# All low halves of expert and u-table pages, and the index one-hot products, on VectorE

## The chip, the cores and the metric

The program runs on one core of a Trainium2 chip. The metric is the device time of one execution in microseconds (us), from the first to the last instruction; less is better. The engines are named as in the profile: PE is TensorE's matmuls and PEld its weight loads, DVE is VectorE, ACT is ScalarE, POOL is GpSimd, SP is SyncE, which issues most DMAs.

## The reference

Two layers on 512 tokens of 1024 features, in float32 (cut to what the change touches):

```python
# layer 1, second half: mixture of 32 experts, 4 for each token
def expert_block(args):
    xe, e = args
    gu = xe @ w_gate_up[e] + b_gate_up[e]
    g = jnp.minimum(gu[:, :D_FF], SWIGLU_LIMIT)
    u = jnp.clip(gu[:, D_FF:], -SWIGLU_LIMIT, SWIGLU_LIMIT)
    act = (u + 1.0) * (g * jax.nn.sigmoid(SWIGLU_ALPHA * g))
    return act @ w_down[e] + b_down[e]
...
# layer 2, second half: 8 heads, 16 of 128 * 128 small experts for each head of a token
cand_i = (i_top[..., 0, :, None] * PEER_KEYS + i_top[..., 1, None, :]).reshape(bsz, seq, PEER_HEADS, PEER_TOPK * PEER_TOPK)
best_s, pos = lax.top_k(cand_s, PEER_TOPK)
expert_idx = jnp.take_along_axis(cand_i, pos, axis=-1)
gates = jax.nn.softmax(best_s, axis=-1)
...
u_sel = u_tab[i_blk]
act = jax.nn.gelu(jnp.einsum('td,thkd->thk', h_blk, u_sel).astype(jnp.float32))
w = (g_blk * act).astype(h.dtype)
return jnp.einsum('thk,thkd->td', w, v_tab[i_blk])
```

Before and after these stand attention layers and a state-space branch, which the change doesn't touch.

## The kernel before

All weights come as pages of 128 x 1024 float32 (512 KB). A product of two float32 matrices is made of three matmuls on halves that the matrix engine takes exactly: `WStream` (L196) loads a page `wr` by a DMA on SP, ACT writes its high half `wh` (`split1`, L217), and another engine writes the low half, `wl = wr - wh` (`low`, L232). The stream's argument `eng` says which engine that is for page number i; None is VectorE. `mm3` (L167) multiplies high by high, high by low and low by high. `get` (L265) hands out the next pair, loads ahead and splits ahead, so that for each page used one later page is split.

**Expert stage** (`phase2`, L1375). 32 places of the stream follow each other, 24 pages to a place (16 of gate and up, 8 of down): 768 pages in order of use (`expert_stream`, L1349). Loops run over the place `e`, over three parts of 8 pages and over the page; a table `sched` puts the other work (gathering an expert's rows, transposing them, the activation `swiglu`, the output `y`) after given pages. `gu` and `dn` are the products' PSUM tiles. The low half of every sixth page goes to GpSimd (L1372). GpSimd also issues the gather of the rows (`xg`, L1244) and the scatter of the results (`ybuf`, L1317).

**U-table stage** (first part of `phase4`, L2213). For three of four blocks of tokens (384 tokens) every small expert's product is made: 128 pages of the u table, 24 matmuls each (`uchunk`, L2297; PSUM tile `ft`, then a gelu on ACT into `us`, which is stored). Between them stand 16 pages of the queries, the choice of the best pairs (`select`, L2320), and `gates` (L2387): from the chosen indices `rt` it builds one-hot matrices `oa` and `oB` on DVE (and one part of `oB` on ACT) whose product `G` spreads the gates over the table; a step of it is 4 tokens, and there are 96. In `select` the position of each best pair is turned into a one-hot tensor `oh`, multiplied with the candidates' indices `ci` (128 x 800), and summed into `ex`. For the last block of tokens the rows are gathered instead (`gathered`, L2445, tiles `ug`, sums in `x`), by indirect DMAs on GpSimd.

The order of these lanes is set by `race` (L99): a `Clock` (L33) adds up estimated costs of what has been emitted for each engine, and the lane that comes due first emits its next step. `Clock.either` (L42) picks VectorE or GpSimd by that estimate and a bias (`VB`, `VB2` = 4.0, 1.0 us against VectorE, L1018); it chose the engine for the low halves of u pages (L2238) and for the product of `oh` and `ci` (L2352). As soon as `race` is over, the last 11 u pages are emitted, then the v-table stage (`vphase`, L2504), in which GpSimd multiplies the stored products by the gates (`gst`).

Of the kernel before, what the change touches and what calls it, by code (L numbers as in the profile page):

```python
# [32 lines left out]
class Clock:  # L33
    """Estimates when each engine gets done with what has been emitted for it; race() orders the steps of several lanes by it."""
# [7 lines left out]
    def either(self, n, bias=0.0):  # L42
        """the one of VectorE and GpSimdE that gets done first with so many columns"""
        cost = [max(self.free[e], self.floor) + self.FIXED[e] + n * self.ELEM[e] for e in ("vector", "gpsimd")]
        return "vector" if cost[0] + bias < cost[1] else "gpsimd"
# [17 lines left out]
class Timed:  # L63
    """An engine whose instructions are told to the clock."""
# [34 lines left out]
def race(clock, *gens):  # L99
    """Interleaves lanes, the step that comes due first first. A lane may yield the time its next step has to wait for;  # L100
    else that is the end of its last step."""
    clock.start()
    live = [[0.0, i, g] for i, g in enumerate(gens)]
    idle = 0
    while live:
        lane = min(live, key=lambda t: (t[0], t[1]))
        clock.floor, clock.end, n = lane[0], lane[0], clock.count
        try:
            t = next(lane[2])
        except StopIteration:  # L110
            live.remove(lane)
            continue
        idle = 0 if t is not None or clock.count > n else idle + 1
        assert idle < 10000
        if t is not None:
            lane[0] = t
        elif clock.count > n:
            lane[0] = clock.end
        else:
            lane[0] = max(lane[0], min([o[0] for o in live if o is not lane], default=0.0)) + 0.01  # L120
# [75 lines left out]
class WStream:  # L196
    """Weight pages: loaded ahead, split into exact float32r halves ahead of their use."""
# [34 lines left out]
    def low(self):  # L232
        """the low halves of what has been split."""
        for eng, r, hi, lo in self.pending:
            eng.tensor_tensor(out=lo, in0=r, in1=hi.bitcast(F32), op=ALU.subtract)
        self.pending = []
# [9 lines left out]
    def lane(self, ahead, n=None):  # L246
        """splits as a lane of its own, so many pages ahead of the use."""
        while self.isp < (n or len(self.srcs)):
            while self.isp > self.ig + ahead:
                yield  # L250
            while self.il < min(len(self.srcs), self.isp + self.la):
                self.load()
            self.late = True
            self.split1()
            yield
            self.low()
            yield

    def next(self):
        """get(), when it has been split."""  # L260
# [15 lines left out]
def weave(*gens):  # L276
    """gens: (generator, steps per unit of time, start); interleaves their steps."""
# [28 lines left out]
def phase1(K):  # L306
# [36 lines left out]
    # first modulation by blocks of columns, so that the first products start early  # L343
# [24 lines left out]
    # row norms of x, the scaled rows' transpose  # L368
# [14 lines left out]
    def mod_block(k):  # L383
        """sum over the rows of w_ada of one block of columns, shift and scale."""
# [54 lines left out]
    def product(bs, k, w):  # L439
        """one row block's part of a half chunk: two blocks of tokens to a bank."""  # L440
# [8 lines left out]
    def normed(c, half):  # L449
        """queries and keys with their heads' norms."""  # L450
# [19 lines left out]
    def drain(c, half, bs):  # L470
        """bs: the blocks of tokens in PSUM, pairs of them or one with all columns."""
# [22 lines left out]
    def take(**n):  # L494
        """waits until so much of the space is free, in the order of the program."""
# [23 lines left out]
    # the first chunk, as the blocks of the modulation come in  # L519
# [37 lines left out]
    def prep(c0, p, out):  # L557
        """q^T and k^T of a pair of heads of 64, split; the gains go with q."""
# [20 lines left out]
    def scores(qk, biases, den, es):  # L579
        """exponentials of the scores of two heads, less each row's maximum, and their sums."""  # L580
# [29 lines left out]
    def weigh(todo, new):  # L610
        """todo: per head its exponentials, the split values' columns, and PSUM [query, block, columns] or the output's place."""
# [50 lines left out]
    def out_pair(b, k, r=slice(0, P)):  # L662
        """a pair's output, transposed in PSUM, split for the output projection."""
# [9 lines left out]
    def pair_a(p):  # L673
# [25 lines left out]
        # each head with the values of both; its own half of the rows is kept  # L699
# [78 lines left out]
    def mods2():  # L778
        """gate and second modulation as rows, broadcast over the partitions."""
# [50 lines left out]
    # output projection: first with the differential heads, then with the others  # L830
# [30 lines left out]
    def projects():  # L861
        """output projection: the differential heads' part, that of the first pairs of the others, and what is left with the second norm"""
# [25 lines left out]
    def third(tb):  # L888
        """the last part of the projection, the residual's squares"""
# [42 lines left out]
    def second(tb):  # L932
        """second norm, router"""
# [39 lines left out]
    def prefetch():  # L973
        """space for the routing and the experts' first weights, as pages come free"""
# [57 lines left out]
def route_start(K):  # L1032
    """constants and space of the routing"""
# [7 lines left out]
    # what the slots of an expert need of a token: its place among the (token, choice) pairs, the gate, a one  # L1041
# [7 lines left out]
def route(K, tb, bank, done):  # L1049
    """top-4 experts of a block of tokens, their gates, and each token's rank within its expert."""  # L1050
# [48 lines left out]
def route_counts(K):  # L1099
    """counts of all tokens, for the experts with more than CAP of them"""  # L1100
# [12 lines left out]
def places(K):  # L1113
    """the expert that each place of the stream serves: the last one from FIXED on with more than CAP tokens, and
    expert HOME, change places; place HOME serves two blocks of CAP slots. What the places need, in their order."""
# [50 lines left out]
def overflow_tables(K):  # L1166
    """further blocks of CAP tokens of an expert: their list, and what each needs, in DRAM."""
# [48 lines left out]
class Expert:  # L1216
    """one block of CAP slots of one expert, in pieces that the caller orders."""
# [113 lines left out]
def load_bias(K):  # L1331
    """biases of all experts: rows 0..31 the high halves, rows 32..63 the low ones; gate and up apart."""
# [16 lines left out]
def expert_stream(K, nexp):  # L1349
    """the experts' weights, in the order of their use"""  # L1350
# [21 lines left out]
    K.ws = WStream(K, srcs, MLA[0], 3, eng=lambda i: K.nc.gpsimd if i % 6 == 5 else None)  # L1372
# [117 lines left out]
class Overflow:  # L1490
    """the blocks that no place of the stream serves, one after the other."""
# [49 lines left out]
def down_bias(K):  # L1541
    """x1 += gate2 * (gates @ b_down)"""
# [23 lines left out]
def expert_rows(K):  # L1566
    """the experts' rows of the tokens, loaded"""
# [10 lines left out]
def combine(K, tb, ys, ssq):  # L1578
    """x2 = x1 + the gated expert rows, and its sums of squares"""
# [13 lines left out]
MAGIC = 12582912.0  # 1.5 * 2**23: rounds a float32 to an integer  # L1593


def exp_exact(K, x, new):
    """exp to float32's accuracy on the vector engine (small tensors); 0 where it underflows."""
# [19 lines left out]
    # times 2**n, in two halves so that both powers are normal numbers  # L1617
# [12 lines left out]
def cmul(K, eng, oc, os_, a, b, tmp):  # L1630
    """(oc, os) = a * b, complex; a, b pairs of access patterns of one shape."""
# [9 lines left out]
NTL = 16  # tiles of 2 groups x 64 states  # L1641


def ssm_params(K):
    """discretization: decay, powers of the rotation, and block-diagonal B (transposed, split) and C."""
# [71 lines left out]
    # block diagonals: [(g, p), tile, (g, h)]  # L1717
# [21 lines left out]
    # powers of the rotation: e^(i theta b), b < 16, and e^(i theta 16 a), a < 32  # L1739
# [17 lines left out]
def ssm_scan(K, uT, yT):  # L1757
    """states of all groups by real scans in the rotating frame, and gelu(C s + d u), transposed."""
# [17 lines left out]
    for c in range(4):  # L1776
        yc = K.small([P, T], tag="yc", bufs=1)
        for i4 in range(4):
# [24 lines left out]
            # the states: cos zr - sin zi, sin zr + cos zi  # L1803
# [30 lines left out]
def norm_T(K, x, gcol, outs, scratch_gain=True):  # L1834
    """row norms of x (token rows), times the gain, transposed and split: outs[k] = (hi, lo) of [128 d, 512 t]."""
# [20 lines left out]
def phase3(K):  # L1856
# [128 lines left out]
    # forget gates: log sigmoid and its running sum, rows 0..7 and again 32..39  # L1985
# [65 lines left out]
    def attn(half, hh):  # L2051
        """one head of the pair"""
# [92 lines left out]
    def gate(j):  # L2145
        """the attention's gates go where its output will, the ssm's wait for it"""
# [54 lines left out]
# pairs (a, b) of the two sorted halves that can be among the 16 largest sums: (a + 1) (b + 1) <= 16  # L2201
# [5 lines left out]
ND = 3  # token blocks whose experts all go through the tensor engine; the last block gathers its experts' rows  # L2207
# [5 lines left out]
def phase4(K):  # L2213
# [24 lines left out]
    ws = WStream(K, [(flat if c else feat)(n) for c, n in order], 3, 2, eng=lambda i: getattr(nc, K.clock.either(D, VB)) if order[i][0] else None)  # L2238
# [66 lines left out]
    def firsts():  # L2305
        """the queries with their 16 best keys of each half, and the first products."""
# [13 lines left out]
    def select(tb, out, h0=0, nh=NH):  # L2320
        """the 16 best pairs of each head: their experts and gates."""
# [25 lines left out]
        for h in range(nh + 1):  # L2347
            if h < nh:
# [3 lines left out]
                getattr(nc, K.clock.either(TK * NCAND, VB2)).tensor_tensor(out=oh, in0=oh, in1=ci[:, h, None, :].to_broadcast(sh), op=ALU.mult)  # L2352
# [34 lines left out]
    def gates(tb, rt):  # L2387
        """G[i, j, token] of a block of tokens, by one-hot products, to DRAM."""
# [56 lines left out]
    def gathered():  # L2445
        """the last block of tokens: rows of its experts, gathered."""
# [99 lines left out]
def host_layout(inp):  # L2546
# [49 lines left out]
    # constants of the shapes: distance penalties and, for the dilated mixture, how often a pair occurs in it  # L2596
# [48 lines left out]
```

## Time and profile before

| | before |
|---|---|
| median of 3 runs | 3914.66 us (3913.98 to 3925.19) |
| span of the profiled execution | 3917.8 us |
| DVE busy | 3368.7 us, 86% |
| PE busy | 3450.1 us, 88% |
| POOL busy | 1761.6 us, 45% |
| expert stage, about | 490 to 1850 us |
| u-table stage, about | 2470 to 3390 us |
| v-table stage, about | 3390 to 3918 us |

The profiled execution is one run of the program; its own time is its span, and the median is that of three others. Busy is the time in which an engine had an instruction at work. An instruction that waits inside for something the profile has no record of counts as busy all the while, so its duration has to be compared with that of its fellows of the same form.

### The profile page before, as it was taken

What the parts mean: (1) busy time and instruction counts of PE and PEld (TensorE: products, weight loads), DVE (VectorE), ACT (ScalarE), POOL (GpSimd) and SP (SyncE); (2) the same over time, 40 slices, a digit from 0 to 9 for tenths busy, and PEclk for the clock granted to TensorE, in tenths of its full rate; (3) what the DMA queues carried; (4) which work ended last, traced back from release to release, by engine and by line L of the source; (5) the groups of instructions that cost most, each with busy time, mean ns of one, the idle gap of its engine ahead of it and who ended that gap; (6) DMA issues with size and microseconds to landing.
All of it is one profiled execution on the core that took longest, in us unless ns stands there. A gap on an engine that the chain in (4) does not pass through costs nothing. (4 is left out here: it accounts for less than half of the span.)

```text
span 3917.8 us, 52046 instructions
## 1 busy us (share of the span) xinstructions
PE 3450.1 (88%) x17053; PEld 2921.3 (75%) x17053; DVE 3368.7 (86%) x5450; ACT 1848.5 (47%) x2684; POOL 1761.6 (45%) x1021
## 2 busy tenths in 40 slices
PE   6887689888989999998489899899688889999999
PEld 6776577666778777776377777788678789988887
DVE  7887799999997999997688774589999996598888
ACT  3334266665765767675234343433334445333333
POOL 6554434323332333332344340266666564555554
PEclk8878799999999999999699999899888999999999
DMA  6224379888987999997511122366568686999997
GB/s 213 85 83 146 127 263 316 299 301 282 321 293 245 320 338 328 338 330 254 175 49 49 49 61 89 124 220 214 187 209 262 210 298 211 328 343 340 344 342 264
DMA packets 453989, 906.04 MB, mean 231 GB/s; under 512 B 37810, under 2 KB 188978, under 8 KB 453586
## 3 DMA queue, kind: packets, MB, share of 16 engines
q1 hardware_dynamic: 333488, 692.66, 52.1%
q0 software_dynamic: 46368, 151.03, 11.0%
q10 hardware_dynamic: 73858, 59.00, 4.5%
q8 instruction: 135, 2.21, 0.2%
q14 instruction: 140, 1.15, 0.1%
HBM read 845.42 MB, written 74.96 MB: 235 GB/s over the span
## 5 line engine op out<-in xcount | busy, mean ns | idle before, releaser
L84 DVE TENSOR_TENSOR wl<-wr,wh 128x1024 fp32r<-128x1024 f32 x855 | 1210.4, 1445 | 113.9 <-ACT wh L84 106.5
L84 ACT CAST wh<-wr 128x1024 fp32r<-128x1024 f32 x1133 | 1133.3, 1049 | 206.1 <-POOL wl L84 53.4
L84 POOL TENSOR_TENSOR wl<-wr,wh 128x1024 fp32r<-128x1024 f32 x278 | 714.3, 2570 | 809.8 <-ACT wh L84 695.1
L84 PE MATMUL ft<-HT,wh 128*128 128x384 f32 (+1 forms) x2304 | 637.6, 359 | 2.4 <-ACT wh L84 2.0
L84 PE MATMUL gu<-wl,exh 128*128 128x512 f32 x1056 | 426.9, 404 | 88.1 <-DVE wl L84 81.6
L84 PE MATMUL out<-wh,HT 128*128 128x512 f32 x1536 | 473.2, 389 | 1.8 <-ACT HT L84 1.5
L84 PEld LDWEIGHTS ft<-HT,wh 128*128 128x128 f32 x2304 | 438.8, 200 | 12.5 <-ACT wh L84 2.4
L84 PE MATMUL ft<-HT,wl 128*128 128x384 f32 (+1 forms) x1152 | 409.6, 356 | 34.6 <-POOL wl L84 24.0
L84 PE MATMUL gu<-wh,exh 128*128 128x512 f32 x1056 | 423.6, 401 | 0.0
L84 PE MATMUL gu<-wh,exl 128*128 128x512 f32 x1056 | 417.4, 395 | 0.0
L84 PEld LDWEIGHTS out<-wh,HT 128*128 128x128 f32 x1536 | 288.2, 188 | 62.3 <-ACT HT L84 1.8
L84 PEld LDWEIGHTS gu<-wl,exh 128*128 128x128 f32 x1056 | 201.3, 191 | 162.8 <-DVE wl L84 116.0
L84 PE MATMUL out<-wl,HT 128*128 128x512 f32 x768 | 298.8, 389 | 0.0
L84 PEld LDWEIGHTS ft<-HT,wl 128*128 128x128 f32 x1152 | 228.6, 198 | 46.9 <-POOL wl L84 28.6
L84 DVE TENSOR_SCALAR oa<-iota,rt 128x128 f32<-128x128 f32 x384 | 227.1, 595 | 19.8 <-PE G L84 19.6
L84 PE MATMUL qkv<-wl,hTh 128*128 128x256 f32 (+1 forms) x736 | 227.1, 308 | 14.5 <-DVE wl L84 11.9
L84 PE MATMUL qkv<-wh,hTh 128*128 128x256 f32 (+1 forms) x736 | 234.7, 319 | 2.0 <-ACT wh L84 2.0
L84 PEld LDWEIGHTS gu<-wh,exh 128*128 128x128 f32 x1056 | 201.6, 191 | 44.5 <-issue 1.5
L84 PEld LDWEIGHTS gu<-wh,exl 128*128 128x128 f32 x1056 | 201.3, 191 | 39.9
L84 PE MATMUL qkv<-wh,hTl 128*128 128x256 f32 (+1 forms) x736 | 226.2, 307 | 2.5 <-DVE hTl L84 2.5
L84 PE MATMUL dn<-wl,ath 128*128 128x512 f32 x528 | 210.2, 398 | 11.0 <-DVE wl L84 9.6
L2454 POOL DMA_INDIRECT ug<-in_peer_v,et x128 | 153.9, 1202 | 139.5 <-DVE x L84 74.0
(482 smaller groups left out, 7054.1 us busy)
## 6 DMA issues: line engine op xcount, KB each, us to landing
wr<-in_w_gate_up SPq DMA_DIRECT2D x512, 512.0 KB
wr<-in_w_down SPq DMA_DIRECT2D x256, 512.0 KB
wr<-in_u_t SPq DMA_DIRECT2D x128, 512.0 KB
wr<-in_peer_v SPq DMA_DIRECT2D x128, 512.0 KB
wr<-in_w_in SPq DMA_DIRECT2D x68, 512.0 KB
wada<-in_w_ada SPq DMA_DIRECT2D x48, 512.0 KB
Sd<-us ACTq DMA_DIRECT2D x128, 192.0 KB
Gd<-gst ACTq DMA_DIRECT2D x12, 2048.0 KB
```

Source lines behind the costliest of these rows:

```text
L84: return f(*a, **kw)
L2454: nc.gpsimd.indirect_dma_start(out=r, out_offset=None, in_=tab, in_offset=bass.IndirectOffsetOnAxis(ap=et[:, m:m + 1], axis=0), bounds_che ...
```

## The change

The low halves of all pages of the expert stream and of the u-table stream, and the 28 products of `oh` and `ci` that had gone to GpSimd, are given to VectorE. Docstrings and comments are taken out as well, with line numbers kept.

```diff
@@ expert_stream
-    K.ws = WStream(K, srcs, MLA[0], 3, eng=lambda i: K.nc.gpsimd if i % 6 == 5 else None)
+    K.ws = WStream(K, srcs, MLA[0], 3)
@@ phase4
-    ws = WStream(K, [(flat if c else feat)(n) for c, n in order], 3, 2, eng=lambda i: getattr(nc, K.clock.either(D, VB)) if order[i][0] else None)
+    ws = WStream(K, [(flat if c else feat)(n) for c, n in order], 3, 2)
@@ select
-                getattr(nc, K.clock.either(TK * NCAND, VB2)).tensor_tensor(out=oh, in0=oh, in1=ci[:, h, None, :].to_broadcast(sh), op=ALU.mult)
+                v.tensor_tensor(out=oh, in0=oh, in1=ci[:, h, None, :].to_broadcast(sh), op=ALU.mult)
```

In the built programs GpSimd's row count falls from 1038 to 759: 251 low halves (128 of the expert stage, 123 of the u table) and 28 products are gone from it and stand on VectorE. GpSimd keeps its DMA issues in both stages.

On DVE, in the expert stage, at the start of a place's list of tokens (`tok` ends it; a line with + is new). Numbers at the end of a name only tell buffers apart:

```order
 L84 TENSOR_SCALAR tok_4472<-dst_4470 128x1
 L84 TENSOR_TENSOR wl_4478<-wr_4261,wh_4477 128x1024
+L84 TENSOR_TENSOR wl_4490<-wr_4278,wh_4489 128x1024
 L84 TENSOR_TENSOR wl_4502<-wr_4295,wh_4501 128x1024
 L84 TENSOR_TENSOR wl_4514<-wr_4309,wh_4513 128x1024
```

The sixth page's low half now stands between its neighbours; nothing else moves in this stage.

On DVE, in the u-table stage of the kernel before, where the one-hot tensors of a block of tokens begin (`bpf` holds the positions):

```order
L84 ISA ug_26725,sv_22824<-ug_26725,ht_22044 128x1024
L84 ISA sv_22824 128x1
L84 CAST bpf_26852<-bp_26851 128x128
L84 TENSOR_TENSOR oh_27062<-bpf_26852,iotac_21953 128x800
L84 TENSOR_SCALAR oa_27065<-iota_21951,rt_26016 128x128
L84 TENSOR_SCALAR oB_27066<-iota_21951,rt_26016 128x128
```

On DVE at the same place of the changed kernel:

```order
L84 TENSOR_TENSOR wl_27271<-wr_27063,wh_27270 128x1024
L84 CAST bpf_27100<-bp_27099 128x128
L84 TENSOR_TENSOR oh_27305<-bpf_27100,iotac_21953 128x800
L84 TENSOR_TENSOR oh_27305<-oh_27305,ci_27026 128x800
L84 ISA ug_26973,sv_22896<-ug_26973,ht_22044 128x1024
```

The product of `oh` and `ci` follows its one-hot tensor, and a low half `wl` stands once for each u page in DVE's queue among the steps of `gates` and `gathered`.

On ACT, the end of `gates` in the kernel before (`gst<-G` empties one step's product, `us<-ft` is the gelu of a u page, and `wh<-wr` is the high half of a page two ahead):

```order
L84 COPY gst_21958<-G_29848 128x4x32x4
L84 COPY gst_21958<-G_29854 128x4x32x4
L84 CAST wh_29860<-wr_29705 128x1024
L84 ACTIVATE us_29891<-ft_29866 128x384
L2301 DMA Sd<-us_29891 128x384
L84 COPY gst_21958<-G_29894 128x4x32x4
L2413 DMA Gd<-gst_21958 4096x1x128
L84 CAST wh_29901<-wr_29756 128x1024
L84 ACTIVATE us_29932<-ft_29907 128x384
```

On ACT, the end of `gates` in the changed kernel:

```order
L84 COPY gst_21958<-G_29984 128x4x32x4
L84 ACTIVATE oB_29991<-iota_21951,rt_28029 128x128
L84 ACTIVATE oB_29991<-oB_29991 128x128
L84 COPY gst_21958<-G_30001 128x4x32x4
L84 ACTIVATE oB_30008<-iota_21951,rt_28029 128x128
L84 ACTIVATE oB_30008<-oB_30008 128x128
L84 COPY gst_21958<-G_30018 128x4x32x4
L84 COPY gst_21958<-G_30024 128x4x32x4
L84 COPY gst_21958<-G_30030 128x4x32x4
L2413 DMA Gd<-gst_21958 4096x1x128
```

The order of the lanes has moved: before, a u page stands between most steps of `gates` up to the last, and 16 u pages follow the last step on PE; now the last ten steps follow each other with no u page between, and 12 pages are left behind them. In front of the first step of `gates` the changed kernel has 20 u pages in a row after the last query page, where there were 16.

## Rows read from the trace of the kernel before

**Rows 1.** The page's first line.

```profile
span 3917.8 us, 52046 instructions
```

**Rows 2.** Windows: busy us by engine (instructions), clock, DMA share, GB/s.

```profile
1300.00:1400.00 100.00, 94.86 (x440) 76.98 (x439) 98.29 (x106) 72.00 (x84) 36.83 (x16) 1.00 0.96 337
3400.00:3500.00 100.00, 100.00 (x443) 82.81 (x442) 91.82 (x90) 37.63 (x52) 58.49 (x48) 1.00 0.97 346
```

**Rows 3.** Windows by stage; columns PE, PEld, DVE, ACT, POOL, clock, DMA, GB/s.

```profile
490.00:1850.00 1360.00, 1247.01 (x5555) 990.62 (x5554) 1291.35 (x1597) 897.75 (x1036) 460.70 (x198) 0.98 0.88 304
2690.00:3260.00 570.00, 470.52 (x2547) 449.41 (x2546) 559.28 (x1172) 224.81 (x424) 369.21 (x206) 0.90 0.71 232
3260.00:3325.00 65.00, 65.00 (x423) 65.00 (x422) 39.13 (x94) 35.09 (x69) 30.13 (x13) 1.00 0.66 202
3340.00:3380.00 40.00, 40.00 (x233) 40.00 (x232) 17.25 (x14) 14.30 (x20) 22.52 (x15) 1.00 0.91 316
```

**Rows 4.** Groups by form on DVE, 490 to 1850: busy us, mean ns.

```profile
L84 DVE TENSOR_TENSOR wl<-wr,wh 128x1024 fp32r<-128x1024 f32 x637 | 900.8, 1452 | 20.1 <-ACT wh L84 17.2 <-DMA ybuf<-y,dst 1.8
L84 DVE SCALAR_TENSOR_TENSOR act<-swu,swt 128x512 f32<-128x512 f32 x66 | 80.2, 1214 | 3.1
L84 DVE SCALAR_TENSOR_TENSOR swt<-gu,swr 128x512 f32<-128x512 f32 x66 | 45.1, 684 | 2.4 <-ACT swr L84 2.4
```

**Rows 5.** Tile views, DVE, 490 to 1850: duration min/median/max in ns.

```profile
L84 DVE TENSOR_TENSOR wl<-wr,wh x637: 1202/1214/3441, 492.0 to 1843.9; 128x1024 fp32r<-128x1024 f32 x160
L84 DVE SCALAR_TENSOR_TENSOR act<-swu,swt x66: 691/1494/2949, 507.4 to 1836.9; 128x512 f32<-128x512 f32 x66
```

**Rows 6.** Groups by form on POOL, 490 to 1850.

```profile
L84 POOL TENSOR_TENSOR wl<-wr,wh 128x1024 fp32r<-128x1024 f32 x128 | 344.1, 2689 | 516.6 <-ACT wh L84 473.8 <-PE dn L84 15.7 <-PE gu L84 14.2
```

**Rows 7.** Timeline of DVE in one place: start, us for the run.

```profile
1440.77 11.31 DVE L84 TENSOR_TENSOR wl<-wr,wh 128x1024 fp32r<-128x1024 f32 x6
...
1465.67 4.62 DVE L84 TENSOR_TENSOR wl<-wr,wh 128x1024 fp32r<-128x1024 f32 x4
```

**Rows 8.** Timeline of POOL in the same place.

```profile
1441.41 2.84 POOL L84 TENSOR_TENSOR wl<-wr,wh 128x1024 fp32r<-128x1024 f32 x1 [2.02 <-ACT wh L84]
1448.47 2.53 POOL L84 TENSOR_TENSOR wl<-wr,wh 128x1024 fp32r<-128x1024 f32 x1 [4.22 <-ACT wh L84]
```

**Rows 9.** Groups by form on PE, 490 to 1850.

```profile
L84 PE MATMUL gu<-wl,exh 128*128 128x512 f32 x1056 | 426.9, 404 | 88.1 <-DVE wl L84 81.6 <-POOL wl L84 6.1
```

**Rows 10.** Groups by form on DVE, 2690 to 3325.

```profile
L84 DVE TENSOR_SCALAR oa<-iota,rt 128x128 f32<-128x128 f32 x384 | 227.1, 595 | 19.8 <-PE G L84 19.6 <-ACT rt L84 0.2
L84 DVE TENSOR_SCALAR oB<-iota,rt 128x128 f32<-128x128 f32 x288 | 163.5, 568 | 0.0
L84 DVE SCALAR_TENSOR_TENSOR x<-ug,sv,x 128x1024 f32<-128x1024 f32 x53 | 85.0, 1604 | 0.5
L84 DVE TENSOR_TENSOR oh<-bpf,iotac 128x800 f32<-128x800 f32 x26 | 33.5, 1292 | 0.8
```

**Rows 11.** Tile views, DVE, 2690 to 3325: duration min/median/max in ns.

```profile
L84 DVE TENSOR_SCALAR oa<-iota,rt x384: 327/336/3260, 2787.2 to 3312.1; 128x128 f32<-128x128 f32 x192
L84 DVE TENSOR_SCALAR oB<-iota,rt x288: 267/275/3254, 2787.5 to 3311.9; 128x128 f32<-128x128 f32 x144
L84 DVE SCALAR_TENSOR_TENSOR x<-ug,sv,x x53: 1259/1279/4073, 2733.0 to 3316.9; 128x1024 f32<-128x1024 f32 x53
L84 DVE TENSOR_TENSOR oh<-oh,ci x4: 991/992/992, 2743.9 to 2777.2; 128x800 f32<-128x800 f32 x4
```

**Rows 12.** Groups by form on POOL, 2690 to 3325.

```profile
L84 POOL TENSOR_TENSOR wl<-wr,wh 128x1024 fp32r<-128x1024 f32 x92 | 225.7, 2455 | 82.7 <-ACT wh L84 47.8 <-issue 25.3 <-PE G L84 8.3
L84 POOL TENSOR_TENSOR oh<-oh,ci 128x800 f32<-128x800 f32 x22 | 44.7, 2033 | 61.1 <-DVE oh L84 58.0 <-DMA wr<-in_u_t 3.0
```

**Rows 13.** Waits of PE, then of ACT, 2690 to 3325: us, times, longest.

```profile
PE G L84 <- DVE oB L84: 62.4, 37, 4.0
...
ACT us L84 <- PE ft L84: 158.6, 61, 8.0
```

## The prediction

> **What bounds the kernel now.** I read the windows first, to see which engine is full in the two stages that the change touches, then the groups by form for DVE and POOL, then single places in the timeline.
>
> In the expert stage (490 to 1850) DVE is busy 1291 of 1360 us, PE 1247, ACT 898, and the DMA engines 0.88 of the time; in a steady piece of it DVE stands at 98% and the DMAs at 0.96 [rows 2, 3]. PE is the engine that waits: 88 us before the product with a low half, 82 of them for DVE [rows 9]. So DVE bounds the stage, with DMA and PE close behind.
>
> In the u-table stage the stretch from the last query page to the last step of `gates` (2690 to 3325, 635 us) falls in two. Until 3260 DVE is busy 559 of 570 us and PE only 470, at a granted clock of 0.90; after that PE is full and DVE at 60% [rows 3]. PE's longest wait is for DVE's `oB`, 62 us [rows 13]. DVE bounds here too. The 16 u pages behind it are PE's: 233 matmuls in 40 us [rows 3], so 24 of them, one page, take 4.12 us.
>
> Now the question that decides the change: is DVE full of its own work? Its low halves have a median of 1214 ns and a mean of 1452, with a longest of 3441; `act` runs between 691 and 2949 ns, with a mean of 1214 [rows 4, 5]. An elementwise instruction of one shape has no reason of its own to take three times as long. The timeline says what lies beside the long ones. Four low halves with no POOL work beside them take 4.62 us, so one more in a row costs (4.62 - 1.21) / 3 = 1.14 us; six at 1440.8 take 11.31 us, where 1.21 + 5 * 1.14 = 6.9 would do, and in this stretch POOL has two low halves, of 2.84 and 2.53 us [rows 7, 8]. DVE lost 4.4 us to 5.4 us of POOL. `swt`, which reads one operand from PSUM, has a mean of 684 ns, right at the shortest `act` of its size: it loses nothing [rows 4, 5].
>
> The Trainium skill has this as a rule (SBUF — State Buffer, Who interferes with whom): the two engines share a pair of ports, and an instruction of VectorE with two SBUF inputs, or in a mode that uses both ports, and one of GpSimd that reads SBUF block each other for the whole instruction. The trace agrees in kind: the forms that stretch are those with two SBUF inputs (`wl`, `act`) and the single-source `oa` and `oB`. The sum below doesn't take the rule's full length, since by rows DVE loses less than POOL's busy time.
>
> **The change part by part.**
>
> *Expert stage.* What DVE loses to POOL: 637 low halves * (1452 - 1214) ns = 152 us, and 66 `act` * (1214 - 691) = 35 us [rows 4, 5]; 186 us together, smaller groups not counted. POOL's 128 low halves go away [rows 6], so this ends; per POOL page it is 186 / 128 = 1.45 us. What DVE gets: the same 128 at 1.14 us in a row, 146 us. Net on DVE: -40 us. The margin is thin, 0.31 us a page. What keeps the stage from giving more or all of it: from about 1180 to 1290 the place with two blocks makes PE the bound (a small part of the stage), and DMA has room of 0.96 to 0.97 in share, or 337 to 346 GB/s, 2.7%, in its steady part [rows 2]; over 1360 us at most 37 us there, more in the slower pieces, where the mean is 304 GB/s [rows 3]. I take 35 us. Bounds: 10 us if the steady pieces are already DMA's; 60 us if the groups I didn't count lose as much again as `act`.
>
> POOL itself is left with DMA issues, so gathers and scatters stand behind nothing; they are loaded two places ahead, so I give that nothing. If this cover were gone, it would show as DVE or PE waiting for `xg`.
>
> *U-table stage, DVE's own sum.* Lost to POOL in 2690 to 3325: `oa` 384 * (595 - 336) = 99 us, `oB` 288 * (568 - 275) = 84, `x` 53 * (1604 - 1279) = 17, `oh` 26 * (1292 - 992) = 8, where 992 is the product of the same shape [rows 10, 11]; together 209 us, against 92 low halves and 22 products on POOL [rows 12], 1.8 us each. Added to DVE: 92 * 1.14 = 105 us and 22 * 0.99 = 22 us, and, because the order of the lanes moves four u pages from behind the last step of `gates` to before it, 4 * 1.14 = 5 us. Net: -77 us. These four pages no longer stand in PE's tail: 4 * 4.12 = 16 us there. Sum 94 us.
>
> DVE had 635 - 559 - 39 = 37 us of slack in this stretch, nearly all after 3260 where PE is full [rows 3]. It can be used up where DVE is the later one, at most 94 + 37 = 131 us. PE must also fit: its 470 us at clock 0.90 are 423 at full clock; with 65 after 3260 and 16 for the four pages that is 505 us [rows 3], below the 540 to 558 that DVE leaves. I take 100 us, a little over 94 for small groups that I left out.
>
> The low bound is in the queue. ACT makes the high half of a page two ahead behind the gelu of the page before, and the gelu waits for PE: 159 us of such waits [rows 13]. Until now POOL alone stood behind that cast. Now DVE does, in order, with the `oa` and `oB` of the next steps queued behind the waiting `wl`, and PE's `G` waits for those. Where PE runs late DVE can't run ahead. If this takes half of the gain, 50 us are left. The ten steps of `gates` without pages at the end are DVE's: eight of them have their one-hot tensors still to come there, 8 * (4 * 0.34 + 3 * 0.28) = 18 us at most [rows 11], with PE half idle; they are in DVE's sum already.
>
> Before 2690 the query pages stand in a chain with the search for their best keys, which the change leaves alone; I count nothing there. The v-table stage is unchanged.
>
> *Sum.* 3917.8 - 35 - 100 = 3783 for an execution like the profiled one [rows 1]; the median of the runs lies 3 us under it: 3780 us.
>
> **The rivals.**
>
> *The expert stage gives nothing but its slow pieces* (DMA is the bound as soon as DVE is a little faster): gain there 10 us, 3915 - 10 - 100 = 3805 us. For it: 0.96 share in the steady piece. Against: 346 GB/s in the v-table stage at 0.97 [rows 2].
>
> *The queue takes half of the u-table gain*: 3915 - 35 - 50 = 3830 us. For it: ACT's waits for PE [rows 13]. Against: a page is split two ahead, about 10 us of PE's work.
>
> *Slower: DVE's long instructions are not POOL's doing.* Then DVE gets the work and nothing back: 146 us less the small part where PE binds, say 130, and 105 + 22 = 127, so 3915 + 257 = 4172 us. It decides wherever a POOL page costs DVE less than the 1.14 us that the page costs when DVE does it; by rows it costs 1.45 and 1.8. For it: only the thinness of the first margin; with that alone wrong by 0.5 us a page the expert stage would lose 25 us and the whole still gain 75. Against: the paired places in the timelines [rows 7, 8].
>
> The Trainium skill has a sentence on that side (Perfetto Trace Analysis, Optimizing Scalar/DVE Operations): with VectorE saturated, giving work to ScalarE or even GpSimd may make sense. It adds that GpSimd and VectorE share a read port, so that between these two it might not help. By the first half alone this change is a loss; the rows bear out the second.
>
> *No effect.* The built order shows that the work has moved, so only gains lost to waits could give this.
>
> **How the numbers follow.** My forecast 0.58 (own range 3750 to 3800), DMA-bound experts 0.16, queue 0.18, slower 0.05, no effect 0.03. The upper bounds of the gains, 60 and 131 less what PE would not follow, give 3735; the queue case with expert gain at its low bound gives 3915 - 10 - 50 = 3855. So 3735 to 3850 holds about 8 in 10. A measurement tells about 0.3%, 12 us, from no change. Faster takes the first three cases but for the worst of the queue: 0.91; the same 0.03; slower 0.06.
>
> **What would show it.** Right: DVE's low halves with a mean near 1.22 us in the expert stage, `act` near 0.69, `oa` and `oB` near 0.34 and 0.28; the stage some 35 us shorter with the DMAs at 0.97 or more; the stretch up to the last step of `gates` near 550 us with PE's clock nearer to 1.0, and 12 u pages behind it at 4.1 us. In the v-table stage, where POOL keeps its arithmetic, `wl` still stretches. Wrong: DVE waiting long for ACT's `wh` in the u-table stage (queue); the expert stage no shorter with DVE below 95% (DMA or PE); means above 1.4 us with POOL idle (the slow rival).

## The result, and the profile after

The changed kernel takes 3761.39 us (median of 4 runs, 3758.15 to 3767.79) against 3914.69 us for the kernel before beside it: a ratio of 0.960, 95% interval 0.9589 to 0.9614. That is 153 us less, where 135 were forecast; 3761 lies inside the own range of the likeliest case. All medians below leave out one execution of 4786.18 us, of the run with the old order of the lanes, whose granted clock was 0.65 where it is 0.94 in its others.

The profile page of the changed kernel begins thus; POOL has gone from 45% busy to 29%, and DVE, which took over 279 instructions, has become less busy in microseconds, not more (3368.7 before).

```profile
span 3762.0 us, 51865 instructions
## 1 busy us (share of the span) xinstructions
PE 3390.4 (90%) x17053; PEld 2884.7 (77%) x17053; DVE 3237.6 (86%) x5729; ACT 1845.3 (49%) x2684; POOL 1096.1 (29%) x742
```

The windows of the changed kernel: the expert stage, a steady piece of it, and the u-table stage from the first u page behind the last query page to the last step of `gates` (columns as in [rows 3]).

```profile
490.00:1780.00 1290.00, 1227.56 (x5546) 984.67 (x5545) 1223.84 (x1721) 892.46 (x1031) 135.55 (x69) 0.99 0.90 320
1300.00:1400.00 100.00, 99.89 (x467) 81.93 (x466) 99.48 (x128) 73.98 (x88) 12.25 (x6) 1.00 1.00 367
...
2609.00:3177.00 568.00, 509.70 (x3036) 497.44 (x3035) 509.61 (x1369) 262.67 (x498) 147.92 (x107) 0.96 0.78 260
```

In the same hundred microseconds PE makes 467 matmuls in place of 440 and DVE 128 instructions in place of 106 [rows 2]. Both are now full there, and the DMAs move 367 GB/s, where 346 was the most that I had found.

The groups by form on DVE, expert stage, and the tile view of `wl` (duration min/median/max in ns): the stretching is gone; no `wl` takes longer than 1228 ns.

```profile
L84 DVE TENSOR_TENSOR wl<-wr,wh 128x1024 fp32r<-128x1024 f32 x763 | 891.2, 1217 | 23.7 <-ACT wh L84 20.7 <-DMA ybuf<-y,dst 1.5 <-issue 1.1
L84 DVE SCALAR_TENSOR_TENSOR act<-swu,swt 128x512 f32<-128x512 f32 x66 | 45.7, 692 | 2.6
L84 DVE SCALAR_TENSOR_TENSOR swt<-gu,swr 128x512 f32<-128x512 f32 x66 | 45.0, 682 | 1.2 <-ACT swr L84 1.2
```

```profile
L84 DVE TENSOR_TENSOR wl<-wr,wh x763: 1201/1217/1228, 490.6 to 1774.4; 128x1024 fp32r<-128x1024 f32 x191
```

PE's wait before the product with a low half falls from 88 us [rows 9] to 22.5:

```profile
L84 PE MATMUL gu<-wl,exh 128*128 128x512 f32 x1053 | 415.9, 395 | 22.5 <-DVE wl L84 22.3
```

The groups on DVE in the u-table stage, 2609 to 3180, which answer to [rows 10]: `oa` from 595 to 359 ns, `oB` from 568 to 290, `x` from 1604 to 1276.

```profile
L84 DVE TENSOR_SCALAR oa<-iota,rt 128x128 f32<-128x128 f32 x384 | 136.7, 359 | 0.0
L84 DVE TENSOR_TENSOR wl<-wr,wh 128x1024 fp32r<-128x1024 f32 x95 | 115.6, 1217 | 55.7 <-ACT wh L84 55.3
L84 DVE TENSOR_SCALAR oB<-iota,rt 128x128 f32<-128x128 f32 x288 | 83.4, 290 | 0.0
...
L84 DVE SCALAR_TENSOR_TENSOR x<-ug,sv,x 128x1024 f32<-128x1024 f32 x50 | 63.8, 1276 | 0.2
L84 DVE TENSOR_TENSOR oh<-oh,ci 128x800 f32<-128x800 f32 x26 | 25.8, 992 | 0.9
```

In the v-table stage, where POOL keeps its arithmetic, `wl` still stretches, as forecast, and the stage still lasts 528 us (3234 to 3762). Groups on DVE, 3240 to 3760:

```profile
L84 DVE TENSOR_TENSOR wl<-wr,wh 128x1024 fp32r<-128x1024 f32 x125 | 180.0, 1440 | 13.8 <-ACT wh L84 11.5 <-issue 1.6
```

Where the 156 us between the two profiled executions come from, by landmarks of the two traces: about 5 lie ahead of the expert stage (its first product comes at 490.0 before and 485.3 after; in the other runs at 481.5 to 490.3, so this is scatter); the stage itself gives 66 (1361.9 us before and 1295.5 after, first product to last); from its end to the first u page behind the last query page 11 (839 and 828); from there to the last step of `gates` 63 (631 and 568); behind it 11, since 12 pages (57 us) stand there and not 16 (68 us).

DVE's busy time in the expert stage, taken from its first product to its last, fell by 64 us, nearly all of what the stage gives. The windows, before and after:

```profile
490.00:1851.90 1361.90, 1248.90 (x5562) 991.85 (x5560) 1292.00 (x1598) 897.75 (x1036) 460.70 (x198) 0.98 0.88 304
485.30:1780.80 1295.50, 1233.02 (x5562) 988.67 (x5560) 1228.26 (x1726) 896.95 (x1036) 136.54 (x70) 0.99 0.90 319
```

What is left in the u-table stage is a new picture: PE and DVE are each about 90% busy and neither is full. The waits there, 2609 to 3177: DVE's, then two of ACT and the longest of PE.

```profile
DVE wl L84 <- ACT wh L84: 52.4, 16, 10.4
...
ACT us L84 <- PE ft L84: 163.2, 74, 6.0
ACT oB L84 <- issue: 58.6, 8, 11.5
...
PE G L84 <- ACT oB L84: 23.3, 6, 8.0
```

### The profile page after: what moved, and what is told of

Read it like the earlier page. It is cut to its first block, busy times and chain, and to the rows that moved or that the text cites. A ratio compares the mean times of both kernels' runs of the same rounds, so it can differ in the third digit from the quotient of the medians.

```text
span 3762.0 us, 51865 instructions
## 1 busy us (share of the span) xinstructions
PE 3390.4 (90%) x17053; PEld 2884.7 (77%) x17053; DVE 3237.6 (86%) x5729; ACT 1845.3 (49%) x2684; POOL 1096.1 (29%) x742
## 3 DMA queue, kind: packets, MB, share of 16 engines
q14 instruction: 139, 1.14, 0.1%
## 5 line engine op out<-in xcount | busy, mean ns | idle before, releaser
L84 DVE TENSOR_TENSOR wl<-wr,wh 128x1024 fp32r<-128x1024 f32 x1106 | 1346.4, 1252 | 150.9 <-ACT wh L84 145.1
L84 PE MATMUL ft<-HT,wh 128*128 128x384 f32 (+1 forms) x2304 | 620.7, 350 | 4.9 <-ACT wh L84 4.9
L84 PE MATMUL gu<-wl,exh 128*128 128x512 f32 x1056 | 417.6, 395 | 22.5 <-DVE wl L84 22.3
L84 PEld LDWEIGHTS ft<-HT,wh 128*128 128x128 f32 x2304 | 424.4, 193 | 14.8 <-ACT wh L84 5.5
L2454 POOL DMA_INDIRECT ug<-in_peer_u,et x128 | 167.6, 1309 | 453.5 <-DVE sv L84 241.5
L1317 POOL DMA_INDIRECT ybuf<-y,dst x33 | 93.3, 2827 | 505.1 <-DVE y L84 505.1
L1244 POOL DMA_INDIRECT xg<-h2d,tok x33 | 42.9, 1300 | 675.8 <-PE dn L84 478.1
```

What stands on the lines that cost most here:

```text
L84: return f(*a, **kw)
L1244: nc.gpsimd.indirect_dma_start(out=self.xg, out_offset=None, in_=K.h2d[:, :], in_offset=bass.IndirectOffsetOnAxis(ap=self.tok[:, :1], axis=0),
L1317: st = nc.gpsimd.indirect_dma_start(out=self.rows, out_offset=bass.IndirectOffsetOnAxis(ap=self.dst[:, :1], axis=0), in_=y, in_offset=None ...
L2454: nc.gpsimd.indirect_dma_start(out=r, out_offset=None, in_=tab, in_offset=bass.IndirectOffsetOnAxis(ap=et[:, m:m + 1], axis=0), bounds_che ...
```

## The experiments

Runs that have a ratio are medians, measured beside the kernel before; the others are single executions, set against 3761.

**The two parts apart.** First the expert stream alone (u pages and products as before), then the u table alone:

```diff
-    ws = WStream(K, [...], 3, 2)                                   # e1_expert_only
+    ws = WStream(K, [...], 3, 2, eng=lambda i: getattr(nc, K.clock.either(D, VB)) if order[i][0] else None)
-    K.ws = WStream(K, srcs, MLA[0], 3)                             # e2_u_only
+    K.ws = WStream(K, srcs, MLA[0], 3, eng=lambda i: K.nc.gpsimd if i % 6 == 5 else None)
```

> Only the expert pages' low halves go to VectorE; u pages and one-hot products stay as they were before. If the two stages gain each on its own, this gives what the traces show between the start and the end of the expert stage, 64 us: 3851 us. If the expert gain were the 35 us of the prediction and the rest came from elsewhere: 3880 us.

> Only the u pages' low halves and the one-hot products go to VectorE; every sixth expert page stays on GpSimd. If the stages are independent: 3915 less 89, 3826 us. If a part of the gain in the u-table stage came from what the expert stage leaves behind: over 3840 us.

Measured: experts alone 3848.08 us, ratio 0.9827 (0.9809 to 0.9845), 69 us less; u table alone 3830.69 us, ratio 0.9771 (0.9749 to 0.9793), 86 us less. Together 155 of 153: the parts add up. The expert term (35) was about half of what this gave, the u-table term (100) too large.

**What of GpSimd's work holds DVE up.** The changed kernel, and beside each sixth expert page one GpSimd instruction of no use, about as long as a low half: once it reads two pages, once it reads one column and then only writes.

```diff
+        nc.gpsimd.tensor_tensor(out=dum, in0=r[:, 0:896], in1=hi[:, 0:896].bitcast(F32), op=ALU.subtract)   # e3_pool_reads
+        nc.gpsimd.tensor_tensor(out=dum[:, 0:1], in0=r[:, 0:1], in1=hi[:, 0:1].bitcast(F32), op=ALU.subtract)   # e4_pool_writes
+        for n in (896, 896, 448):
+            nc.gpsimd.memset(dum[:, 0:n], 0.0)
```

> The changed kernel, and beside VectorE's low half of every sixth expert page GpSimd makes 896 of its 1024 columns once more into a tile that nobody reads. If what counts is that GpSimd's reads hold up VectorE: VectorE keeps all 24 low halves of a place and loses 4 * 1.3 us or more to GpSimd again, so the places go from 36.3 to about 41.5 us and the time to some 3915 us. If what counted was only that PE waited for GpSimd's slow low half: no change, 3761 us.

> As the run with the second low half, but GpSimd reads one column and then writes 2240 columns of zeros, some 2.3 us, with each sixth page. If only GpSimd's reads hold up VectorE's two-operand instructions: VectorE's low halves keep a mean near 1.25 us and the time stays within 10 us of 3761. If any GpSimd work on the memory holds VectorE up: as the other run, some 3900 us.

Measured: 3967.35 us with the reads, 206 more than the changed kernel; 3769.80 with the writes, 8 more. Groups by form of the run with reads, 490 to 1780:

```profile
L84 DVE TENSOR_TENSOR wl<-wr,wh 128x1024 fp32r<-128x1024 f32 x650 | 927.3, 1473 | 9.0 <-ACT wh L84 4.8 <-POOL dum L84 2.1 <-DMA ybuf<-y,dst 0.9
...
L84 POOL TENSOR_TENSOR dum<-wr,wh 128x896 f32<-128x896 f32 x109 | 298.7, 2740 | 466.8 <-ACT wh L84 278.6 <-issue 176.3 <-DMA wr<-in_w_down 10.9
...
L84 DVE SCALAR_TENSOR_TENSOR act<-swu,swt 128x512 f32<-128x512 f32 x57 | 51.1, 897 | 2.2
```

And of the run with writes, same stretch:

```profile
L84 DVE TENSOR_TENSOR wl<-wr,wh 128x1024 fp32r<-128x1024 f32 x760 | 887.9, 1217 | 22.7 <-ACT wh L84 18.1 <-DMA ybuf<-y,dst 2.5 <-PE gu L84 0.9
...
L84 POOL MEMSET dum<- 128x896 f32 x254 | 215.9, 850 | 14.8
...
L84 POOL TENSOR_TENSOR dum<-wr,wh 128x1 f32<-128x1 f32 x127 | 125.9, 991 | 451.8 <-issue 240.2 <-ACT wh L84 209.1 <-POOL dum L84 1.0
```

In the first, the mean of `wl` is back where it was before the change (1473 against 1452 ns) and that of `act` part of the way (897; 1214 before), and (650 * 256 + 57 * 205) ns / 109 = 1.6 us are lost for each of POOL's instructions; 206 / 128 gives the same 1.6. In the second POOL is busy longer, and DVE's mean is 1217 ns as without it. So for `wl` and `act` it is what GpSimd reads, not that it works, that DVE pays for. The Trainium skill says this (SBUF — State Buffer, Who interferes with whom): a VectorE instruction with two SBUF inputs contends with a GpSimd instruction that reads SBUF, and not with one that only writes it. These two runs agree.

For `oa` and `oB`, which have one input, no run sets GpSimd's writes alone beside them. They are still touched a little: between 2609 and 3180 of the changed kernel the 132 `oa` that overlap the issue of a gather on GpSimd take 401 ns in the mean (at most 540), the 252 others 338 (at most 347), while `wl` takes 1217 either way.

**What binds the expert stage now.** Less work for DVE (every sixth low half not made), then less for PE (one of three products left out):

```diff
+            if self.skip and self.isp % 6 == 5:                    # e5_dve_less
+                self.done.append((hi, hi))
-            self.K.mm3(self.gu[i], (...), (...), False, k == KC - 1)   # e6_pe_less, the same for dn
+            for j in range(2):
+                self.K.nc.tensor.matmul(self.gu[i], self.xT[0][:, s], w[j][:, i, :], start=False, stop=j == 1 and k == KC - 1)
```

> The changed kernel, but every sixth expert page has no low half made: the high half stands in for it, so VectorE does 4 of 24 low halves less a place and PE does as much as before. In the steady places of the changed kernel DVE and PE are both busy over 99% and the DMAs 0.96 to 1.00. If DVE alone is the bound there, the place goes from 36.3 towards 31.7 us until PE or DMA holds it, 34 us at least, and the time falls by 60 us or more, to 3700 us. If PE or DMA holds it as much: 36 us a place, 3750 us or more.

> The changed kernel, but in the experts the third product (high half of the weights with the low half of the rows) is left out: PE has a third less to do there, DVE and DMA the same. If DVE or DMA is the bound in the steady places: 36.3 us again, and only the places with two blocks get shorter, 3720 to 3750 us. If PE was the bound: places of 34 us or less, under 3690 us.

Measured: 3718.02 us (43 less) and 3738.01 us (23 less). A steady place lasts 39.3 us before, 36.3 after, 36.0 with less for DVE, and still 36.3 with less for PE. A window of each, first with less for DVE:

```profile
1300.00:1400.00 100.00, 100.00 (x469) 82.95 (x468) 89.31 (x116) 77.22 (x90) 7.80 (x5) 1.00 0.99 362
```

then with less for PE:

```profile
1300.00:1400.00 100.00, 81.91 (x325) 55.49 (x323) 99.33 (x126) 77.36 (x90) 12.43 (x6) 0.97 0.94 353
```

With DVE at 89% PE is full, the DMAs stand at 0.99, and the place is no more than 0.3 us shorter; with PE at 82% DVE is full and the DMAs stand at 0.94. So in a steady place DVE needs 36.3 us, and PE or the DMAs 36.0; which of these two it is, no run separates. What the first run gains comes from elsewhere: its expert stage is 60 us shorter, 56 of them in the first sixteen places (the seventh 49.7 to 42.7 us, the eleventh 46.1 to 41.1), where DVE has more than the pages to do; the u-table stretch, which it leaves alone, took 9 us longer in this execution. In the second the place with two blocks (61.3 to 48.3 us) and the one behind it (47.6 to 43.2) give 17 of the 30 us that its stage is shorter, the early places most of the rest.

**The order of the lanes.** All the work on VectorE, but the clock is told the costs of the engines that had it before, so that PE's order is that of the kernel before:

```diff
+    class told:
+        def tensor_tensor(self, **kw):
+            K.clock.spend(self.name, self.n)
+            return v.eng.tensor_tensor(**kw)
+    ... eng=lambda i: told(K.clock.either(D, VB), D) if order[i][0] else None)
```

> The changed kernel, all low halves and products on VectorE, but the lanes of the u-table stage in the order that the kernel before had (the clock is told the old engine's costs): 16 u pages behind the last step of gates instead of 12, and no burst of ten steps. If the order was worth the 16 us that I counted for the four pages: 3777 us. If the burst of ten steps costs what the shorter tail gains: 3761 us. If the old order lets DVE and PE overlap better: 3745 us.

Measured: 3789.02 us (three executions), ratio 0.9668 (0.9649 to 0.9687), 28 us slower than the changed kernel. PE's instructions are in the order of the kernel before, one by one. Its profiled execution is 31 us longer than that of the changed kernel, and the landmarks say where:

- 11 us stand behind the last step of `gates` (16 pages, 68 us, where the changed kernel has 12 in 57).
- 9 us stand between the end of the expert stage and the first u page behind the last query page. That part takes 837 us here, 838 and 839 in the two other traces with the old order (experts alone, and the kernel before), and 827 to 830 in every trace with the new one.
- 7 us stand in the stretch from there to the last step, where PE waits 17.8 us for DVE's `oB`, against 1.1. This is no clear difference: the stretch lasts 563 to 577 us in six traces with the changed kernel's instructions there, and 575 here. The rest lies ahead of the stage's end.

So the shift of lanes, which I had counted as 16 us for four pages and nothing else, is worth some 20 to 28 of the 153.

**The products of `oh` and `ci` alone** back on GpSimd, all of them, in the changed kernel's order:

```diff
-                v.tensor_tensor(out=oh, in0=oh, in1=ci[:, h, None, :].to_broadcast(sh), op=ALU.mult)
+                (K.clock.spend("vector", TK * NCAND), nc.nc.gpsimd)[1].tensor_tensor(out=oh, in0=oh, in1=ci[:, h, None, :].to_broadcast(sh), op=ALU.mult)
```

> The changed kernel in the same order, only the products of oh and ci on GpSimd, all 32 of them. DVE saves 32 * 0.91 = 29 us and loses, if each holds it up as the pages did, 32 * 1.5 = 48 us or more, and its sum waits for GpSimd: 10 to 25 us slower, 3771 to 3786 us. If 1.8 us of GpSimd beside DVE's work cost DVE less than 0.91 us: 3750 us.

Measured: 3772.43 us, ratio 0.9638 (0.9618 to 0.9658), 11 us slower than the changed kernel; the two intervals do not quite meet at 0.9614 and 0.9618. The groups of DVE and of POOL, 2609 to 3180:

```profile
L84 DVE TENSOR_SCALAR oa<-iota,rt 128x128 f32<-128x128 f32 x371 | 140.9, 382 | 0.0
L84 DVE TENSOR_TENSOR wl<-wr,wh 128x1024 fp32r<-128x1024 f32 x94 | 128.4, 1366 | 49.9 <-ACT wh L84 49.6
L84 DVE TENSOR_SCALAR oB<-iota,rt 128x128 f32<-128x128 f32 x278 | 89.9, 323 | 0.0
```

```profile
L2352 POOL TENSOR_TENSOR oh<-oh,ci 128x800 f32<-128x800 f32 x26 | 62.6, 2409 | 86.6 <-DVE oh L84 86.6
```

DVE is rid of 26 * 0.99 = 26 us. But its `oa` and `oB` are slower again, 382 and 323 ns against 359 and 290, which with `x` makes some 21 us, and its low halves, 1366 ns against 1217, another 14. So it loses 35 us and gains 26; the 9 us between them are near the 11 measured.

**Is it ACT's queue?** The low bound of the prediction was that ACT's cast `wh` stands behind a gelu that waits for PE. So the gelu was put one page later in ACT's queue; and, since that would do nothing where the order of the lanes is at fault, the pace of the u pages was changed so that no burst of steps is left at the end; then both.

```diff
-        b = chunk(TD)                                              # e9_late_gelu, e11_late_pace55
+        made.append((j, chunk(TD)))
+        if len(made) > 1:
+            gelu()
-    UPACE, BV = 5.1, 3                                             # e10_pace55, e11_late_pace55
+    UPACE, BV = 5.5, 3
```

> The changed kernel with the gelu of each u page one page later in ACT's queue, so that the high half of a page two ahead stands in front of the gelu that waits for PE, and VectorE's low half no longer waits behind it. DVE waits 55 us for the high halves in the u-table stage of the changed kernel. If this queue is what kept the stage's gain under what DVE's sum allowed: these waits fall under 20 us and the time by 15 to 40 us, to 3720 to 3745 us. If DVE only waited there while PE was the bound anyway: the waits fall and the time stays within 8 us of 3761.

> The changed kernel with the u pages paced at 5.5 us instead of 5.1 us of the clock: 17 u pages are left behind the last step of gates instead of 12, and the burst of ten steps is gone. If only DVE's sum and the tail count: five pages more in PE's tail, 21 us, less five low halves before it, 6 us: 3776 us. If the burst, in which PE is half idle, is what the order costs: 3750 us.

> Both edits. If each acts on its own: the sum of their two differences from the changed kernel, within 8 us. If the later gelu takes away the waits that make the order matter: as the later gelu alone.

Measured: 3769.32 us (ratio 0.9613, 0.9593 to 0.9633), 3761.02 (0.9596, 0.958 to 0.9612) and 3759.78 (0.9596, 0.958 to 0.9612): nothing gained. DVE's waits for `wh`, which were to fall under 20 us if the gelu's place made them, stayed at 58 us (2609 to 3170 of the first run). ACT's waits in that run, 2609 to 3177:

```profile
ACT gst L84 <- PE G L84: 99.1, 48, 3.8
ACT oB L84 <- issue: 76.9, 8, 13.1
ACT wh L84 <- PE ft L84: 34.8, 11, 6.6
```

ACT now waits for PE in front of `gst`, where it had waited in front of `us`; whichever comes first in its queue is the one that waits. But the second row stayed and grew: waits that the profile puts down to issue. Since they grew in the same run, it doesn't show what the gelu's place is worth without them.

**One DMA issue moved.** ACT's timeline in the changed kernel shows what that is (start, us; ACTq rows are DMA issues):

```profile
3057.32 0.55 ACTq L2413 DMA_DIRECT2D Gd<-gst  x1
3057.97 1.05 ACT L84 CAST wh<-wr 128x1024 fp32r<-128x1024 f32 x1 [0.67 <-DVE sv L84]
3060.87 0.49 ACT L84 ACTIVATE us<-ft 128x384 f32<-128x384 f32 x1 [1.85 <-PE ft L84]
3061.39 11.43 ACTq L2301 DMA_DIRECT2D Sd<-us  x1
3072.87 0.40 ACT L84 ACTIVATE oB<-iota,rt 128x128 f32<-128x128 f32 x1 [11.51 <-issue]
```

The store of a block of gates, 4096 rows of 512 bytes, is issued in 0.55 us; the next issue in the same queue, a small store that takes 0.33 us elsewhere, takes 11.43, and ACT stands still. Ten such issues before the last step of `gates` take 62.8 us; in the kernel before there were seven, 30.4 us, and in the run with the later gelu ten, 86.9 us. The edit gives the large store to SP:

```diff
-                    nc.scalar.dma_start(out=Gd[tb, :, :, g * GT:(g + 1) * GT, :], in_=st)
+                    nc.sync.dma_start(out=Gd[tb, :, :, g * GT:(g + 1) * GT, :], in_=st)
```

> The changed kernel with one more edit: the store of a finished block of gates, Gd<-gst (4096 rows of 128 floats), is issued on SyncE in place of ScalarE. PE's order is the same. In the changed kernel the issue of a store Sd<-us that comes right behind such a store takes 3.29 us (at 2756.91) where others take 0.33, and ScalarE idles 58.6 us before oB that the profile puts down to issue (2609 to 3180). Theory A (these stalls of ScalarE are what keeps VectorE and TensorE below full in the u-table stage): the 58.6 us fall below 35, PE's waits for ScalarE's oB (23 us) below 10, and the time to 3741 to 3752 us. Theory B (they lie beside other waits, or come back on SyncE's queue as late pages): the issue idle falls, but the time stays within 8 us of 3761, or rises.

Measured: 3731.52 us (3724.04 to 3732.76), ratio 0.951 (0.9485 to 0.9535): 30 us less than the changed kernel, and the shortest of all the runs that leave no work out. The issues of this run, 2609 to 3177 (duration min/median/max in ns):

```profile
L213 SPq DMA_DIRECT2D wr<-in_u_t x100: 327/328/11852, 2618.5 to 3176.0; - x100
L2301 ACTq DMA_DIRECT2D Sd<-us x100: 326/326/373, 2615.0 to 3176.5; - x100
```

and of the changed kernel:

```profile
L213 SPq DMA_DIRECT2D wr<-in_u_t x93: 327/328/328, 2618.5 to 3158.2; - x93
L2301 ACTq DMA_DIRECT2D Sd<-us x94: 326/326/11432, 2615.2 to 3164.7; - x94
```

The long issue has not gone; it has moved to whoever issues behind the large store. On SP that is a load of a page three pages ahead of its use, and little waits for it. The window up to the last step of `gates`, which now comes at 3144, not 3177 (535 us, where the six traces named above have 563 to 577), and the waits of DVE and PE in it:

```profile
2609.00:3144.00 535.00, 499.35 (x3032) 487.80 (x3032) 509.09 (x1369) 262.43 (x498) 147.91 (x107) 0.98 0.82 276
```

```profile
DVE wl L84 <- ACT wh L84: 20.7, 11, 5.0
...
PE ft L84 <- DVE wl L84: 19.2, 20, 2.0
PE r4T L84 <- DVE r L84: 15.4, 3, 6.6
PE G L84 <- DVE oB L84: 1.1, 2, 0.6
```

PE's wait for ACT's `oB` is gone, DVE's for `wh` is less than half, and DVE is busy 95% of the stretch. The 21 us of waits for `wh` that are left are the most that the gelu's place can still cost DVE here. It costs a little elsewhere: ACT waits 15.6 us, four times, for a page that comes late.

## Why the prediction was right

The forecast was faster, 3780 us; the mechanism held, and two terms of the sum were off, with opposite signs. That 3761 lies as near to 3780 as it does is in part luck: the expert term was some 30 us too small, the u-table term 14 too large, and 26 too large for the stretch and tail that it was worked out for.

- *DVE is not full of its own work.* Right. The means of `wl`, `act` and `x` fell to the medians or shortest durations of the trace before, those of `oa` and `oB` to within 25 ns of the medians, and GpSimd's reads bring the stretching back where its writes don't (3967 us against 3770). The slower rival would have needed 4172.
- *What DVE loses for one of POOL's pages, 1.45 us.* A little low. Counted against the changed kernel's means, `wl` lost 637 * (1452 - 1217) ns = 150 us, `act` 34, and the smaller groups that I left out about 20 more: some 205 us, or 1.6 a page.
- *Expert stage, 35 us.* The mis-sized term: it measured 66 to 69, above its upper bound of 60. DVE's busy time alone fell by 64 us (1292.0 to 1228.3), not 40: the low halves took 8 us less in all, though 128 more of them were DVE's, `act` 34 less and the smaller groups 21. And the cap that I set on DVE's gain was wrong. I held the DMAs to the 346 GB/s and the share of 0.97 that the v-table stage showed; with DVE faster they moved 367 at a share of 1.00 over the hundred microseconds above and 359 at 0.98 over nine steady places, and 362 with DVE at 89%. A share of 0.96 was what the engines had been asked for, not what they could.
- *U-table stage, 100 us.* The run of the u table alone gave 86, but 11 of these lie ahead of the stretch that the term was worked out for; the stretch gave 63, not 84, and the tail 11, not 16. DVE's own sum did better than forecast: 598.4 us busy in 635 before [rows 3], 509.6 in 568 after, 89 less where I had 77. But its idle time, which I thought could be used up, grew from 37 to 58 us, and 52 of these are the waits for `wh`. The 12 pages behind took 57 us, not 12 * 4.12 = 49, with PE for 20 us at a granted clock of 0.91.
- *Its low bound, "in the queue".* One of the prediction's own signs of being wrong did show: DVE waited for `wh`, 52 us. The reason was only partly the one given. The stalled issues behind `Gd` were 63 us, twice those of before; with the store moved to SP the waits fall to 21 us and the stretch to 535, below the 540 to 558 that I had for DVE's share. Moving the gelu gained nothing, but in a run where the stalls were longer, so its part stays open.
- *Four u pages out of PE's tail, 16 us.* The tail gave 11; the new order as a whole is worth 20 to 28.
- *Before 2690, nothing.* About 11 us came from there. 24 of the u table's low halves had been on POOL before that point too, but that is not the reason: with these on DVE and the old order of the lanes the part is as long as before (837 us, 839 before, 828 after). It came with the order.
- *The v-table stage unchanged, and the gathers behind nothing.* Right: 528 us, and PE and DVE wait for no `xg`.

## What to carry to other kernels

Where an instruction of one shape takes three times as long at its longest as at its shortest, and no row names what it waits for, look at what the neighbouring engine does in those microseconds, and price that engine's help by what it costs the engine helped (here 1.6 us lost for 1.14 us of work taken over). A busy share under 1.00 on DMAs that follow the compute tells what they were asked for; it is a poor cap on a forecast. And look at which queue a large store of small rows is issued from: here the next issue behind it stalled for up to 11 us, which cost little on the engine that loads ahead, and 30 us on the one that feeds two others.

## What the runs showed of the hardware

- GpSimd's reading and writing differ altogether for VectorE's instructions with two inputs in SBUF: in the whole runs, 352 us of GpSimd instructions that read two pages cost 206 us, 405 us of instructions that nearly only write cost 8.
- The issue of a DMA of 192 KB behind a store of 4096 rows of 512 bytes in the same queue took 1.5 to 11.4 us in the changed kernel; with the store on SP, the issue of a page load took up to 11.9. Elsewhere either takes 0.33 us. The Trainium skill says (DMA: Bandwidth & Descriptors, Issuing engines are not separate DMA queues) that DMAs from several engines share the same 16 DMA engines, and that issuing from more than one only saves the issuer's time, usually small beside the transfer. No run here tests the first half. As to the second, the issuer's time was not small here: moving one store's issue gained 30 us. Why the issue takes so long no run here shows.
- One core's DMAs moved 367 GB/s over 100 us of the changed kernel's expert stage, and 359 over nine places of it.
